# ScalarE's splits that are prepared behind a visit's turnings, queued behind the copies of the turned blocks (hybrid SSD and forgetting-attention layer)

## The chip, the cores and the metric

The kernel runs on one core of a Trainium2 chip. The metric is the device time of one execution in microseconds (us). Five engines work side by side, each with an instruction queue of its own: TensorE (PE, with its weight loads shown apart as PEld), VectorE (DVE), ScalarE (ACT), GpSimd (POOL) and SyncE (SP), which here only issues DMAs. ACT and POOL issue DMAs too. Engines wait for each other through semaphores. The order of the instructions within each queue is fixed when the program is built: a scheduler with a model of the instructions' times plays the program through and puts the instructions in the order in which they come up in that play.

## The reference

One decoder layer on 1024 tokens of width 1024, all in float32, with an SSM branch and an attention branch that share one input projection:

```python
h = rmsnorm(x) * pre_g
z_ssm, xbc, dt, q, k, v, f, z_att, g_ssm, g_att = split(h @ w_in)
# branch A: causal convolution, chunked SSD scan, gated group norm -> y_ssm
# branch B, 16 heads of 64, in blocks of 128 queries:
s = q @ k.T / 8 + F[t] - F[s]          # F = cumsum(log_sigmoid(f)), causal
o = softmax(s) @ v
y_att = o * silu(z_att)
merged = sigmoid(g_ssm) * (y_ssm @ w_branch_ssm) + sigmoid(g_att) * (y_att @ w_branch_att)
out = x + rmsnorm(merged @ w_out) * post_g
```

## The kernel before

**The projections are one long stream.** Every large product (input columns, the two branch matrices, `w_out`) is cut into pairs of units (`Pair`), and each pair is computed by seven half-size products instead of eight, with sums and differences of blocks as operands. One such product is a *step*: twelve matmuls of 128x128 by 128x512, six to each *half-step*. A matmul takes fp32 through two pieces: a high part that ACT makes by copying (`AF.Copy`) and a low part that DVE makes by subtracting the high part. This is what the text calls a *split*. The weights' split is `Pair.split` (ACT at line 351, DVE at line 352, tile `wop`, four buffers). The split of the other operand is `Operands.split` (ACT at 277 or 280, DVE at 278 or 281, tiles `x0h`, `x0l` and so on).

**`Stream` deals the steps out.** `Stream.half()` (line 530) issues one half-step. When the half begins a step, it first calls `ahead(False)`, which prepares the weights of the step three places on (`prepare`, line 522: sums on DVE or POOL, then the split). After the half, each operand set under construction gets a call of `some()` (lines 556 to 560), which fetches blocks and splits those that have landed. Between `hold()` and `release()` these calls are put aside and made later.

**Attention runs between the half-steps.** There are 48 *visits* (`for m in range(6 * NK)`): eight pairs of heads, six visits each. A visit has these parts, and PE takes them in just this order, since its instructions are all kept in program order: the scores (`scores`, tile `s` in PSUM); the weighted sums of the visit before (`weighted`, tile `av`); one or two half-steps "ahead"; the turnings (`turned`, line 1475: PE transposes the probabilities `ex` into PSUM tiles `pt`); and one or two half-steps "behind" (three in the last visit). On the other engines the visit has DVE's addition of the forget term with a row minimum (line 1467, `ex` and `nm`), ACT's exponentials (1471), and the copies of the turned blocks from PSUM into `p` (ACT at 1510, one of four on DVE at 1508 for the first six pairs of heads). `weighted` reads `p`. Scores and turned blocks share one ring of four PSUM buffers (tag `s`), so the next visit's scores need the copies of this visit to be done.

**What sets ACT's order.** Three things bear on it. Instructions under `tc.high_priority()` (the copies at 1510, the exponentials, `Pair.keep` at 404, `give` at 412) go first among those that are ready in the scheduler's play. Instructions under `pin` stay in program order among themselves; the exponentials and the operands' splits are pinned, the weights' splits and the copies are not. And a buffer must be free: a weights' split takes one of four `wop` buffers, and so comes up when the step four places earlier has left PE.

The pass over a visit, cut to the calls that order the work (lines 1648 to 1681):

```python
for one in made:
    weighted(*one)
...
stream.release()
...
stream.halves(ahead)
...
made = turned(hp, g, list(end(m - 1)))
...
stream.hold()
stream.halves(behind)
```

Of the kernel before, what the change touches and what calls it, by code (L numbers as in the profile page):

```python
# [11 lines left out]
AF = mybir.ActivationFunctionType  # L12
# [74 lines left out]
def hybrid_layer(ctx: ExitStack, tc, a, out):  # L87

    nc = tc.nc
# [366 lines left out]
    class Stream:  # L456
# [6 lines left out]
        def __init__(self, pairs, double, last):  # L463
            self.pairs = pairs
            for n, p in enumerate(pairs):
                p.bank, p.other = (pj, "be"[n % 2]), (pjx, "d") if n < double else (pj, "c")

                p.between = n < double or n >= last

            p, q, r = pairs[0:3]  # L470
            self.steps = [(p, 1), (q, 1), (p, 2), (q, 2)] + [(p, n) for n in (6, 5, 7, 4, 3)]
            self.steps += [(q, 6), (q, 5), (q, 7), (r, 1), (q, 4), (q, 3)]
            for n in range(2, last):
                p, nxt = pairs[n], pairs[n + 1]
                self.steps += [(p, i) for i in ((2, 6, 5, 7) if n < double else (6, 2, 7, 5))] + [(nxt, 1)]
                self.steps += [(p, 4), (p, 3)] if n + 1 < last else [(p, 3), (p, 4)]

            a, b, c, d, e, f, g, h = pairs[last:]
            self.steps += [(a, 5), (a, 6), (a, 7), (b, 1), (a, 2), (a, 4), (a, 3)]
            for p, nxt in ((b, c), (c, d), (d, e)):  # L480
                self.steps += [(p, 2), (p, 6), (p, 5), (p, 7), (nxt, 1), (p, 4), (p, 3)]
            self.steps += [(f, 1), (e, 2), (e, 6), (e, 5), (e, 7), (f, 2), (e, 4), (e, 3)]
            self.steps += [(f, 6), (f, 5), (f, 7), (g, 1), (f, 4), (f, 3)]
            self.steps += [(g, 2), (g, 6), (g, 5), (g, 7), (h, 1), (g, 4), (g, 3)]
            self.steps += [(h, 6), (h, 5), (h, 7), (h, 2), (h, 3), (h, 4)]
            self.following = {p: n.ops for p, n in zip(pairs, pairs[1:]) if n.ops is not p.ops}
            self.building = []
            self.chores, self.line = [], []
            self.held = None
            self.count = 0  # L490
            self.at = 0
            self.run = None
            self.waiting = []
            self.loads = [(p, names) for p in pairs for names in (("a11", "a12"), ("a21", "a22"))]
            self.loaded = []
            self.load_next()
# [23 lines left out]
                self.prepare(p, which)  # L520

        def prepare(self, p, which):
            p.prepare(which)
            self.load_more()

        def after(self, halves, fn):

# [2 lines left out]
        def half(self):  # L530
            if self.run is None:
                if self.at == len(self.steps):
                    return False
                p, which = self.steps[self.at]
                if which == 7 and p.ops is ops_a and "merged" not in fin:
                    return False
                if p.ops is ops_a and not all(p.ops.ready(OPERAND[which].strip("-"), j) for j in range(KH)):
                    return False
                self.ahead(False)
                for ops in self.building:  # L540
                    ops.some(OPERAND[which])
                self.run = p.do(which)
                next(self.run)
            else:
                for _ in self.run:
                    pass
                self.run = None
                p, which = self.steps[self.at]
                if p in self.following:
                    ops = self.following[p]  # L550
                    if ops not in self.building:
                        self.building.append(ops)
                    ops.open(OPERAND[which])
                self.ahead(True)
                self.at += 1
            for ops in self.building:
                if self.held is None:
                    ops.some()
                else:
                    self.held.append(ops)  # L560
            for chores in (self.chores, self.line):
                if chores:
                    chore = chores.pop(0)
                    if chore:
                        chore()
            self.count += 1
            for w in self.waiting:
                w[0] -= 1
            for w in [w for w in self.waiting if w[0] <= 0]:
                self.waiting.remove(w)  # L570
                w[1]()
            return True
# [4 lines left out]

        def release(self):
            held, self.held = self.held or [], None
            for ops in held:  # L580
                ops.some()

        def do_chores(self):
            while self.chores:
# [550 lines left out]
    with tc.tile_pool(name="pro", bufs=1, reuse_waits="tile", side="right") as pro, tc.tile_pool(  # L1135
# [53 lines left out]
        stream = Stream(order + late + ends, len(order) + 3, len(order) + len(late) + 4)  # L1189
# [105 lines left out]
    with tc.tile_pool(name="att", bufs=1, reuse_waits="tile", side="right") as ap, tc.tile_pool(  # L1295
# [177 lines left out]
        def turned(hp, g, sent):  # L1473

            pair, h = GROUPS[g]
            bs = list(range(4 * h, min(4 * h + 4, pair[0] + 1)))
            made = {}  # L1480
            order = bs[-1:] + bs[:-1] if sent else bs
            tiles = {b: pp.tile([P, HALF], F32, tag="s", bufs=4, name="pt") for b in order}
            banks = {b: tiles[b].rearrange("p (e t c) -> p e t c", e=2, t=2) for b in order}

            def turn_one(b, e, t):
                turn(banks[b][:, e, t, :], ex[:, e, 1 - t, b % 4 * P : b % 4 * P + P])

            for e in range(2):
                for b in order:
                    turn_one(b, e, 1)  # L1490
            for b in order:
                bank, first = banks[b], max(b - pair[1], 0)
                if sent and b == bs[-1]:
                    assert first == 1
                    for hd, which in sent:
                        hd.turn(which, tiles[b])
                if not first:
                    for e in range(2):
                        turn_one(b, e, 0)
                if sent and b == bs[-1]:  # L1500
                    for hd, which in sent:
                        hd.send(which, tiles[b])
                p = ap.tile([P, 2, 2, P], F32, tag="p", bufs=4, name="p")
                to, src = (x[:, :, first:, :] for x in (p, bank))
                with tc.high_priority():

                    if b % 4 == 1 and hp < NK - 2:
                        nc.vector.tensor_copy(to, src)
                    else:
                        nc.scalar.activation(to, src, AF.Copy)  # L1510
                made[b] = (hp, g, b, first, p)
            return [(*made[b], b == bs[0], b == bs[-1]) for b in bs]

# [126 lines left out]
        for m in range(6 * NK + 1):  # L1640

            if m < 6 * NK:
                hp, g = divmod(m, 6)
                if not g:
                    heads[hp] = Heads(hp)
                for u in range(2):
                    scores(hp, g, u)
            for one in made:
                weighted(*one)
            for hd, which in end(m - 1):  # L1650
                hd.free(which)
            if m == 6 * NK:
                stream.release()
                heads[NK - 1].out(2)
                break
            for hd, which in end(m - 2):
                if hd.last and which:
                    hd.out(which)
            for fn in deferred:
                fn()  # L1660
            deferred.clear()
            stream.release()
            for hd, which in end(m):
                hd.settle(which)
            ahead, behind = room(m)
            stream.halves(ahead)

            for hd, which in end(m):
                hd.scale(which)
                hd.load_gates(which)  # L1670
            loads(m)
            made = turned(hp, g, list(end(m - 1)))
            for hd, which in end(m - 2):
                if not hd.last or not which:
                    hd.out(which)
            if m == 6 * NK - 1:
                tp = pp.tile([P, HALF], F32, tag="s", bufs=4, name="tp")
                heads[hp].turn(2, tp)
                heads[hp].send(2, tp)
            stream.hold()  # L1680
            stream.halves(behind)
            for hd, which in end(m if m == 6 * NK - 1 else m - 1):
                hd.take(which)
# [59 lines left out]
```

## Time and profile before

| what | value |
| --- | --- |
| median of 3 runs | 1290.88 us (1290.15 to 1292.31) |
| the profiled execution, its own time | 1291.84 us |
| its span, first to last instruction | 1290.1 us |
| mean granted TensorE clock | 0.996 |
| attention's 48 visits | from 686.8 to about 1135 us of the span |

The profiled execution is 0.96 us (0.07%) above the median of the runs, and 1.7 us of its time lie outside its span. In the profile, "busy" leaves out the time in which an instruction waits; "idle before" a group is what its engine waited, with the releaser that ended most of it. A matmul's end is modelled, so PE counts as busy from one matmul to the next where they follow closely. The timeline merges equal neighbours into one row (x4 is four instructions) and gives the start, the length, the engine, the line, and the tiles as output<-input.

### The profile page before, as it was taken

The page shows a single profiled execution, that of the slowest core. Times are in us where ns is not written, and L with a number is a line of the kernel's source. Part 1 is how long each engine was busy: PE and PEld are TensorE (multiplying, and loading weights), DVE is VectorE, ACT ScalarE, POOL GpSimd, SP SyncE. Part 2 cuts the span into 40 slices and gives each one's busy share as a digit, 9 for nine tenths or more (in the row PEclk, how much of TensorE's full clock was granted, in tenths as well). Part 3 has the DMA queues.
Part 4 walks back from the last instruction along what each step waited for, and adds up shares of the span by engine and source line. Part 5 has one row for each costly group of instructions (what it writes and reads, how often), then busy time and mean ns, then how long its engine had stood idle before and what let it go on. Part 6 is the DMA issues. An engine that isn't in the chain of part 4 may idle for free.

```text
span 1290.1 us, 20992 instructions
## 1 busy us (share of the span) xinstructions
PE 1255.2 (97%) x7054; PEld 987.4 (77%) x7054; DVE 1005.1 (78%) x1994; ACT 795.6 (62%) x1738; POOL 258.8 (20%) x250
## 2 busy tenths in 40 slices
PE   5999999999999999999999999999999999899997
PEld 3688888787888888888877777777777776678886
DVE  7988886987788978997767567666798767776975
ACT  7745665556665665566556666666786567644754
POOL 4000440013300330124101121110001102146052
PEclk9999999999999999999999999999999999999999
DMA  8232552646336533653365666667787568556932
GB/s 297 72 113 76 154 154 90 190 150 182 131 110 201 186 126 105 217 168 119 132 204 202 200 222 204 206 215 224 259 261 249 199 212 268 191 188 195 360 111 101
DMA packets 153515, 233.57 MB, mean 181 GB/s; under 512 B 15968, under 2 KB 61504, under 8 KB 153408
## 3 DMA queue, kind: packets, MB, share of 16 engines
q1 hardware_dynamic: 137408, 197.14, 48.0%
q10 hardware_dynamic: 11136, 19.11, 3.9%
q0 software_dynamic: 4864, 15.99, 3.2%
q8 instruction: 55, 0.90, 0.3%
q14 instruction: 52, 0.43, 0.1%
HBM read 162.99 MB, written 72.34 MB: 182 GB/s over the span
## 4 chain that ended last, share of the span: by engine, by line
PE 76%; DVE 8%; DMA 7%; ACT 4%; issue 2%; SPq 1%; ACTq 0%; DVEq 0%
PE pb L130 32%; PE pc L130 19%; PE pd L130 6%; PE s L130 5%; PE pt L133 5%; PE av L130 4%; PE yps L130 2%; DVE wop L352 2%; DMA raw<-in_wu 1%; DMA xt<-in_x 1%; PE st L130 1%; DVE sum L357 1%; DMA st_dram<-st 1%; PE tr L133 1%; PE tr_v L133 1%
## 5 line engine op out<-in xcount | busy, mean ns | idle before, releaser
L351 ACT ACTIVATE wop<-sum 128x512 fp32r<-128x512 f32 x180 | 112.5, 626 | 111.4 <-DVE sum L357 52.3
L352 DVE TENSOR_TENSOR wop<-sum,wop 128x512 fp32r<-128x512 f32 x180 | 137.1, 763 | 55.0 <-ACT wop L351 54.0
L1471 ACT ACTIVATE ex<-ex,nm 128x512 f32<-128x512 f32 (+1 forms) x192 | 116.3, 607 | 65.8 <-DVE nm L1467 62.5
L404 ACT ACTIVATE s<-pb 128x512 f32<-128x512 f32 x144 | 85.2, 591 | 99.7 <-PE pb L130 97.7
L130 PE MATMUL pc<-x3h,wop 128*128 128x512 f32 x384 | 130.6, 397 | 1.6 <-DVE th L414 1.3
L130 PE MATMUL pc<-x2h,wop 128*128 128x512 f32 x384 | 130.7, 398 | 0.6 <-DVE u L416 0.6
L130 PE MATMUL pb<-x0h,wop 128*128 128x512 f32 x384 | 131.0, 399 | 0.0
L130 PE MATMUL pb<-x5h,wop 128*128 128x512 f32 x384 | 129.8, 396 | 1.1 <-ACT s L404 1.1
L130 PE MATMUL pb<-x6h,wop 128*128 128x512 f32 x384 | 129.4, 395 | 1.3 <-ACT s L404 1.3
L352 DVE TENSOR_TENSOR wop<-raw,wop 128x512 fp32r<-128x512 f32 x144 | 101.0, 703 | 36.3 <-ACT wop L351 35.9
L130 PE MATMUL pb<-x4h,wop 128*128 128x512 f32 x384 | 129.2, 395 | 0.0
L1467 DVE CUSTOM_DVE_ANT_0 ex<-s,fb 128x512 f32<-128x512 f32 (+1 forms) x192 | 97.2, 552 | 20.0 <-PE s L130 19.9
L351 ACT ACTIVATE wop<-raw 128x512 fp32r<-128x512 f32 x144 | 89.7, 623 | 21.1 <-PE pc L130 13.6
L130 PE MATMUL pd<-x1h,wop 128*128 128x512 f32 x288 | 96.3, 394 | 0.0
L130 PEld LDWEIGHTS pc<-x3h,wop 128*128 128x128 f32 x384 | 72.3, 188 | 18.9 <-DVE th L414 1.7
L130 PEld LDWEIGHTS pb<-x5h,wop 128*128 128x128 f32 x384 | 72.1, 188 | 18.7 <-ACT s L404 2.2
L130 PEld LDWEIGHTS pc<-x2h,wop 128*128 128x128 f32 x384 | 72.1, 188 | 18.4 <-issue 2.8
L130 PEld LDWEIGHTS pb<-x6h,wop 128*128 128x128 f32 x384 | 72.1, 188 | 18.2 <-issue 1.9
L130 PEld LDWEIGHTS pb<-x0h,wop 128*128 128x128 f32 x384 | 72.7, 189 | 17.3 <-issue 2.7
L130 PEld LDWEIGHTS pb<-x4h,wop 128*128 128x128 f32 x384 | 72.3, 188 | 17.1 <-issue 2.3
L133 PE MATMUL pt<-ident,ex 128*128 128x128 f32 x576 | 75.4, 274 | 1.6 <-DVE nm L1467 0.6
L130 PE MATMUL s<-k,q 64*128 64x512 f32 (+3 forms) x576 | 73.6, 368 | 2.0 <-ACT p L1510 1.5
(310 smaller groups left out, 2915.8 us busy)
## 6 DMA issues: line engine op xcount, KB each, us to landing
raw<-in_wu SPq DMA_DIRECT2D x128, 256.0 KB
csb<-cs_dram SPq DMA_DIRECT2D x32, 256.0 KB
fb<-f_dram SPq DMA_DIRECT2D x16, 512.0 KB
rb<-st_dram SPq DMA_DIRECT2D x48, 128.0 KB
wd<-in_wo SPq DMA_DIRECT2D x40, 128.0 KB
xt<-in_x SPq DMA_DIRECT2D x8, 512.0 KB
gs_dram<-th ACTq DMA_DIRECT2D x16, 256.0 KB
qh_dram<-th ACTq DMA_DIRECT2D x16, 256.0 KB
```

The source lines that it names most:

```text
L130: return tc.keep_in_program_order(nc.tensor.matmul(*args, **kw))
L133: return tc.keep_in_program_order(nc.tensor.transpose(out_, in_, idn))
L351: nc.scalar.activation(op[:, 0], src, AF.Copy)
L352: nc.vector.tensor_tensor(op[:, 1], src, op[:, 0], ALU.subtract)
L357: self.adds.tensor_tensor(t, x, y, ALU.add)
L404: nc.scalar.activation(s, ps, AF.Copy)
L1467: nc.vector.tensor_tensor_reduce(o, s[e][:, 0:w], fb[hp, h][:, e, 0:w], 1.0, 3.0e38, ALU.add, ALU.min, nm)
L1471: pin(nc.scalar.activation(o, o, AF.Exp, scale=-1.0, bias=nm, accum_out=hd.at(hd.sm, i, h, e)))
```

## The change

`Stream` gets a field `front`. In `turned`, each copy that goes to ACT is noted there, so after the turnings of a visit `front` is that visit's last copy on ACT. `Stream.behind()` opens `tc.issue_after(front)`: every instruction that is written inside it on the same engine as `front`, which is ACT, gets an ordering edge to it. That is no semaphore and no wait on the chip; it only keeps the scheduler from putting the instruction ahead of the copy in ACT's queue. Three places are wrapped: the preparation of weights (`prepare`), the calls of `some()` on operands that are not held, and the held ones when they are released. At the end of attention `front` is cleared. The list of held calls holds functions instead of objects. Nothing is computed otherwise, and no instruction, DMA or buffer is added or taken away.

```diff
@@ Stream.__init__
             self.held = None
+            self.front = None
@@ Stream
         def prepare(self, p, which):
-            p.prepare(which)
+            with self.behind():
+                p.prepare(which)
             self.load_more()
+
+        def behind(self):
+
+            return nullcontext() if self.front is None else tc.issue_after(self.front)
@@ Stream.half
             for ops in self.building:
                 if self.held is None:
-                    ops.some()
+                    with self.behind():
+                        ops.some()
                 else:
-                    self.held.append(ops)
+                    self.held.append(ops.some)
@@ Stream.release
             held, self.held = self.held or [], None
-            for ops in held:
-                ops.some()
+            for fn in held:
+                with self.behind():
+                    fn()
@@ turned
                     else:
-                        nc.scalar.activation(to, src, AF.Copy)
+                        copy = nc.scalar.activation(to, src, AF.Copy)
+                        stream.front = copy.ins
@@ the loop over the visits
             if m == 6 * NK:
+                stream.front = None
                 stream.release()
```

## The prediction

> **What bounds the kernel now.** The page comes first: the span, then the engines' shares.
>
> ```profile
> span 1290.1 us, 20992 instructions
> PE 1255.2 (97%) x7054; PEld 987.4 (77%) x7054; DVE 1005.1 (78%) x1994; ACT 795.6 (62%) x1738; POOL 258.8 (20%) x250
> ```
>
> PE is idle for 35 us in all. The change reaches only attention, so the next view is the busy time by stretches: pairs of heads 1 and 3 (counted from 0), then 4, then 7, then a short stretch at the end of pair 7. After the stretch and its length stand the busy time of each engine with its instructions, the granted clock and the DMAs.
>
> ```profile
> core 0: us, PE busy (x) PEld busy (x) DVE busy (x) ACT busy (x) POOL busy (x), PEclk, DMA share, GB/s
> 745.83:803.27 57.44, 57.44 (x393) 43.81 (x391) 38.47 (x102) 36.19 (x91) 10.51 (x13) 1.00 0.67 216
> ...
> 860.58:917.89 57.31, 57.31 (x394) 43.84 (x392) 38.53 (x105) 38.78 (x96) 6.87 (x9) 1.00 0.69 223
> 917.89:969.38 51.49, 50.85 (x357) 37.98 (x355) 46.46 (x122) 43.07 (x107) 2.16 (x4) 1.00 0.83 270
> ...
> 1073.09:1135.00 61.91, 55.69 (x345) 39.69 (x344) 48.14 (x117) 42.20 (x105) 9.54 (x13) 0.94 0.66 216
> ...
> 1130.60:1134.00 3.40, 3.40 (x14) 1.90 (x13) 2.27 (x5) 1.74 (x4) 0.00 (x0) 0.53 0.23 78
> ```
>
> In pairs 1 and 3 PE is busy for all of the stretch, and the two agree within 0.13 us: PE runs at its own pace there, and nothing that ACT does earlier can shorten them. What PE loses lies in pair 4 (0.64 us) and above all in pair 7 (6.22 us). Third come PE's waits (and its weight loads') between 660 or 675 and 1140 us: who waited for whom, total, times, longest.
>
> ```profile
> PE tp L133 <- DVE ns L1376: 3.3, 1, 3.3
> PE s L130 <- ACT p L1510: 1.5, 3, 1.1
> ...
> PEld s L130 <- ACT p L1510: 5.4, 12, 1.5
> ```
>
> The second and third row are what the change is about: scores that wait for the copies to empty a PSUM buffer. The matmuls waited 1.5 us for that, the weight loads 5.4 us, much of which passes while earlier matmuls still run.
>
> **The change part by part.** Only ACT's order can change: nothing is added, so all terms come from places in the queue.
>
> *Operands' splits (L277, L280): nothing.* Those of a visit are written after its exponentials and pinned behind them. The exponentials need scores, and these need the copies of the visit before, whose order the edge is to set; so the timeline has, in each of the 47 transitions, the last copy on ACT before the next visit's first exponential (one pair of such rows stands further down, 886.36 and 888.87). The edge repeats an order that stands. It doesn't even reach the costliest case:
>
> ```profile
> 1115.59 0.62 ACT L351 ACTIVATE wop<-sum 128x512 fp32r<-128x512 f32 x1
> 1116.11 1.14 ACT L280 ACTIVATE x3h<-x3l 128x512 fp32r<-128x512 f32 x2
> 1117.93 0.27 ACT L1393 ACTIVATE st<-pt 8x128 f32<-8x128 f32 x1 [0.69 <-PE pb L130]
> 1118.11 0.36 ACT L1510 ACTIVATE p<-pt 128x256 f32<-128x256 f32 x1
> ...
> 1118.52 1.09 PE L130 MATMUL s<-k,q 64*128 64x256 f32 x6 [1.09 <-ACT p L1510]
> ```
>
> This is visit 46, with PE's longest wait for a copy, 1.09 us. The operands' splits ahead of `st`, and the weights' split between them, were written before this visit's turnings, when `front` still was visit 45's last copy. They stay.
>
> *Weights' splits prepared in the half-steps behind (L351).* I went through the timeline visit by visit. PE's order shows which half-steps behind begin a step, and the n-th split belongs to the n-th step. 31 preparations fall behind the turnings, 48 ahead; none of the 48 stands before the copies of the visit before. Of the 31, 21 started before their visit's last copy on ACT. These are what moves; the other ten run after the copies already. The first and the last of the 21, and one from pair 1:
>
> ```profile
> 692.70 0.62 ACT L351 ACTIVATE wop<-raw 128x512 fp32r<-128x512 f32 x1
> 693.23 1.33 ACT L1510 ACTIVATE p<-pt 128x512 f32<-128x512 f32 x3
> ...
> 759.64 0.63 ACT L351 ACTIVATE wop<-sum 128x512 fp32r<-128x512 f32 x1 [1.08 <-PE pc L130]
> ...
> 760.90 0.58 ACT L1510 ACTIVATE p<-pt 128x512 f32<-128x512 f32 x1
> ...
> 1105.96 0.62 ACT L351 ACTIVATE wop<-sum 128x512 fp32r<-128x512 f32 x1
> 1106.48 0.20 ACT L1368 ACTIVATE dd<-dd 128x8 f32<-128x8 f32 x1
> 1106.58 2.04 ACT L1510 ACTIVATE p<-pt 128x512 f32<-128x512 f32 x4
> ```
>
> The split at 759.64 lies in a hole in which ACT had nothing else, and is over 0.6 us before the copy: moving it gains nothing. In ten of the 21 a copy (or `st`, or `dd`) follows directly, as at 693.23, and could start up to 0.5 us earlier. It gains time only where PE waits for it. In nine of the ten the scores behind run in their usual time (within 0.1 us). The tenth is visit 45; the scores behind it stand here under those of the same group in pair 1:
>
> ```profile
> 781.97 0.96 PE L130 MATMUL s<-k,q 64*128 64x512 f32 x6
> ...
> 783.70 0.65 PE L130 MATMUL av<-p,v 128*64 128x256 f32 x4
> ...
> 1107.41 1.24 PE L130 MATMUL s<-k,q 64*128 64x512 f32 x6
> ...
> 1109.51 1.95 PE L130 MATMUL av<-p,v 128*64 128x256 f32 x16
> ```
>
> From the scores' start to `av` it takes 1.73 us in pair 1 and 2.10 us behind visit 45: a stall of 0.37 us, which copies 0.5 us earlier would cover. **Gain: 0.4 us.**
>
> *What the moved splits meet.* Each can start when the last copy ends: for the first of the rows above at 694.56 instead of 692.70, 1.9 us later, for the last at 1108.62, 2.7 us later. Its DVE half (L352) comes later with it. The weights are used three steps on, behind 36 matmuls at least; at pair 3's pace (57.31 us for 394) that is 5.2 us, an estimate that leaves out what stands between steps, so PE doesn't wait for weights. On ACT the split falls into the hole between copies and exponentials. On DVE it can fall ahead of the next row minima (L1467), on which exponentials and turnings hang. The tightest place is visits 20 and 21:
>
> ```profile
> 886.36 0.60 ACT L1510 ACTIVATE p<-pt 128x512 f32<-128x512 f32 x1 [0.37 <-ACT st L1393]
> 888.87 0.72 ACT L1471 ACTIVATE ex<-ex,nm 128x512 f32<-128x512 f32 x1 [1.92 <-DVE nm L1467]
> ...
> 887.54 0.69 DVE L381 TENSOR_TENSOR raw<-raw 128x512 f32<-128x512 f32 x1
> 888.15 0.68 DVE L1467 CUSTOM_DVE_ANT_0 ex<-s,fb 128x512 f32<-128x512 f32 x1
> ...
> 891.62 0.19 ACT L1471 ACTIVATION_READ_ACCUMULATOR ex<-ex,nm 128x1 f32 x1
> ...
> 892.01 1.25 PE L133 MATMUL pt<-ident,ex 128*128 128x128 f32 x10
> ```
>
> The moved split would run from 886.96 to 887.6, its DVE half beside L381. If that goes before L1467, the minima come 0.6 us later, and of that the exponentials' lead over the turnings (891.71 to 892.01) covers 0.30: a loss of 0.3 us. Ends for this term: 0 if the scheduler puts DVE's half behind the minima (they have priority), and 0.3 us. I take 0.2. The order of DVE and SP follows the scheduler's play too, and the trace can't show that. The nearest rows bound it: SP holds back loads of weights for L352, and DVE stands for ACT's half.
>
> ```profile
> SPq L344 <- DVE wop L352: 28.0, 10, 7.4
> ...
> DVE wop L352 <- ACT wop L351: 39.2, 29, 3.4
> ```
>
> Some 2.7 us at most (the longer of the two moves) is added to each of those ten waits, and loads of `q`, `k` and `rb` stand behind them on SP; PE waits for none of them today but the last `rb`. DVE's 39.2 us may shrink or move, and PE has no wait from them in pairs 0 to 6. I take 0 for both, with 2.7 us of loss and 1 us of gain as ends.
>
> *Sum:* -0.4 + 0.2 = -0.2 us. On the profiled execution that is 1291.84 - 0.2 = 1291.6. That execution stands 0.96 us above the median of the runs, 1290.88, so on the median the sum makes **1290.7 us**, the number I give.
>
> *A rule against my reading.* The stretch of pair 3 has PE 100% busy, and PEld 43.84 of 57.31 us. The Trainium skill (Perfetto Trace Analysis, Identifying the Most-Contended Engine) says that a busy share of matmuls isn't a good measure of how near PE is to its limit and that the share of weight loads is one. By it, PE could have 13 us to give in each pair, and ten copies 0.5 us earlier might be worth 5 us: 1285.9. By the rows it is 0.4, since equal stretches with no wait leave nothing for a copy to release. I go by the rows.
>
> **The rivals.**
>
> *Slower: the moved halves land in the next visit's chain.* DVE's half (0.69) before the minima and ACT's (0.62) before the exponentials delay the turnings by up to 1.31 us. What covers it is the exponentials' lead over the turnings. It is below 0.76 us behind nine of the 21 (visits 2, 8, 12, 14, 20, 27, 36, 38, 45), the first and the last of these:
>
> ```profile
> 719.19 0.19 ACT L1471 ACTIVATION_READ_ACCUMULATOR ex<-ex,nm 128x1 f32 x1
> ...
> 719.95 1.25 PE L133 MATMUL pt<-ident,ex 128*128 128x128 f32 x10
> ...
> 1113.41 0.19 ACT L1471 ACTIVATION_READ_ACCUMULATOR ex<-ex,nm 128x1 f32 x1
> ...
> 1114.25 1.03 PE L133 MATMUL pt<-ident,ex 128*128 128x128 f32 x8
> ```
>
> The lead there is 0.67 and 0.75 us (the next instruction overlaps the read by 0.1). It decides from where both halves come before the last minimum. Price: 9 x (1.31 - 0.67) = 5.8 us, so 1296.7; with half of them 1293.8. For it: DVE is 90% busy in pair 4. Against it: minima and exponentials have priority, and ACT's holes mostly hold the split.
>
> *Faster: the end of pair 7 closes up.* PE stands 3.3 us for `ns` (the first row of its waits), which DVE reaches only after it has waited for `rb`:
>
> ```profile
> 1127.40 0.69 DVE L1431 TENSOR_TENSOR o<-o,rb 128x512 f32<-128x512 f32 x1 [2.99 <-DMA rb<-st_dram]
> ```
>
> That DMA hangs on the `st` of 1117.93. In the stretch from 1130.60 the granted clock is 0.53: just behind the gap PE works at half speed for 3.4 us, a loss of 1.7 us. If the copies of visit 45 and a new order of DVE bring `st` 1 us forward and the gap closes by as much, the half-speed stretch may vanish with it: 0.4 + 1.0 + 1.7 = 3.1 us, so 1287.8. The Trainium skill (TensorE: Matmul & The Clock Gate, What's actually happening) has the clock halved after an idle window of about 3.4 us and given back after a busy one of that length; the trace agrees, with 3.3 us idle and 3.4 us slow. Against it: what holds `st` is not an ACT split that moves.
>
> *Slower by transfers:* a held-back weight load delays the `rb` or `q` behind it in pair 7, up to 2.7 us: 1293.6.
>
> *The edge binds nothing that matters* (the copies start earlier, and PE gives it back at the gap): 1290.9, inside the forecast.
>
> **How the numbers follow.** What can be told from no change is 0.2%, 2.6 us. Forecast, with the last rival: 0.34; its own range 1288.3 to 1293.4. Faster: 0.30. Slower in the next visit's chain: 0.27; by transfers: 0.09. That makes 0.30 faster, 0.34 the same, 0.36 slower. The range goes from 1286.2, below the faster case, to 1296.7, the full price of the slower one.
>
> **What would show it.** Right: no L351 prepared behind stands ahead of the visit's last L1510; the stretches of pairs 1 and 3 keep 57.3 us; the time from scores to `av` behind visit 45 falls to about 1.75 us; the row of PE waiting for `p` keeps its 1.09 us. Slower is shown by new waits of `pt` for L1471 or L1467 in pairs 0 to 6; faster by a shorter wait of `tp`. Wrong is the forecast if PE's order or the length of a stretch before pair 4 changes, or if the stage after attention moves: it has the same instructions and may still be put in another order.

## The result, and the profile after

| | median | runs | ratio, 95% interval |
| --- | --- | --- | --- |
| before, measured beside it | 1290.59 us (1287.28 to 1294.19) | 15 | |
| changed kernel | 1288.41 us (1286.99 to 1290.55) | 15 | 0.9982 [0.9974, 0.9991] |

The change makes the kernel 2.2 us faster (0.18%). Runs of one kernel spread over 3.6 to 7 us, so one profile is never enough to tell such a difference; the medians of many runs do, and the profiles say where to look. In the rows shown, line numbers from 1000 on are 8 higher after than before.

The first view is the page's span and shares, then the busy time by stretches (columns as before: pair 3, pair 7, and the 3.4 us behind the gap at its end), then PE's waits from 675 to 1140 us, all of the changed kernel.

```profile
span 1288.2 us, 20979 instructions
PE 1255.0 (97%) x7054; PEld 987.1 (77%) x7054; DVE 1006.2 (78%) x1994; ACT 795.4 (62%) x1738; POOL 259.5 (20%) x250
```

```profile
859.60:917.00 57.40, 57.40 (x396) 43.89 (x393) 39.44 (x107) 38.61 (x95) 7.17 (x9) 1.00 0.67 222
...
1073.00:1133.60 60.60, 54.67 (x343) 38.95 (x342) 46.28 (x117) 41.86 (x105) 9.39 (x13) 0.94 0.66 223
1128.70:1132.10 3.40, 3.40 (x14) 1.84 (x13) 2.04 (x4) 2.27 (x5) 0.00 (x0) 0.50 0.12 44
```

```profile
PE tp L133 <- DVE ns L1384: 3.3, 1, 3.3
PE pt L133 <- DVE nm L1475: 1.5, 3, 0.9
PE pt L133 <- ACT ex L1479: 0.9, 3, 0.4
PE pb L130 <- ACT s L404: 0.7, 1, 0.7
PE s L130 <- DVE p L1516: 0.3, 1, 0.3
```

PE's busy time is the same. Pair 3 has no idle time, as before. What is gone is the row of scores that waited for ACT's `p` (1.5 us before, 1.09 us of it at visit 46). What is new is 1.5 us of turnings that wait for the row minima (0.6 us before, and all three are in pair 7: from 675 to 1070 us there is no such row). The gap at the end of pair 7 (`tp`) and the half-speed stretch behind it are still there. Another row of before that is gone, 1.3 us in which `pc` waits for `th` (L414) at 675.7 us, lies ahead of attention. It comes and goes between kernels with the same queues up to there (1.6 us in E7 below, none in E9).

Below, a visit's length is the time from the start of its scores to the start of the next scores; for the last one, visit 47, to the turned norms `tp`. From visit 7's scores to visit 24's both traces take 162.04 us, and from visit 0's to visit 42's 383.76 before and 383.87 after. Within the latter, visit 0 takes 9.07 us before and 10.16 after, and pair 4 takes 51.53 and 50.63; a second profile of the changed kernel (E1 below) has 9.36 and 52.03, so neither difference can be put down to the change. What is left is pair 7. There the two profiles differ by 0.8 of the 1.9 us between their spans, which is too little to go by alone.

### The profile page after: what moved, and what is told of

The parts are those of the page before. It is cut to its first block, busy times and chain, and to the rows that moved or that the text cites. A ratio compares the mean times of both kernels' runs of the same rounds, so it can differ in the third digit from the quotient of the medians.

```text
span 1288.2 us, 20979 instructions
## 1 busy us (share of the span) xinstructions
PE 1255.0 (97%) x7054; PEld 987.1 (77%) x7054; DVE 1006.2 (78%) x1994; ACT 795.4 (62%) x1738; POOL 259.5 (20%) x250
## 4 chain that ended last, share of the span: by engine, by line
PE 75%; DVE 9%; DMA 8%; ACT 3%; issue 3%; SPq 1%; POOL 0%; DVEq 0%; ACTq 0%; POOLq 0%
PE pb L130 31%; PE pc L130 18%; PE pd L130 5%; PE pt L133 5%; PE s L130 5%; PE av L130 5%; PE yps L130 2%; DVE wop L352 2%; DMA raw<-in_wu 1%; DVE sum L357 1%; DMA xt<-in_x 1%; DVE xs L779 1%; DMA xr<-in_x 1%; PE st L130 1%; DVE ex L1475 1%
## 5 line engine op out<-in xcount | busy, mean ns | idle before, releaser
L352 DVE TENSOR_TENSOR wop<-sum,wop 128x512 fp32r<-128x512 f32 x180 | 138.0, 768 | 57.5 <-ACT wop L351 56.7
L352 DVE TENSOR_TENSOR wop<-raw,wop 128x512 fp32r<-128x512 f32 x144 | 104.1, 724 | 36.5 <-ACT wop L351 36.0
L130 PEld LDWEIGHTS pc<-x2h,wop 128*128 128x128 f32 x384 | 72.6, 189 | 18.1 <-issue 2.8
L133 PEld LDWEIGHTS pt<-ident,ex 128*128 128x128 f32 x576 | 66.8, 141 | 13.7 <-ACT ex L1479 4.4
```

What stands on the lines that cost most here:

```text
L130: return tc.keep_in_program_order(nc.tensor.matmul(*args, **kw))
L133: return tc.keep_in_program_order(nc.tensor.transpose(out_, in_, idn))
L352: nc.vector.tensor_tensor(op[:, 1], src, op[:, 0], ALU.subtract)
```

## The experiments

The table has all the profiles of pair 7 side by side (us, from the timeline's starts of `s<-k,q` and `tp<-ident,ns`), with the ratio of the times to the kernel before.

| kernel | 42 and 43 | 44 | 45 | 46 | 47 | sum | ratio, 95% interval |
| --- | --- | --- | --- | --- | --- | --- | --- |
| before | 19.21 | 8.11 | 9.56 | 11.10 | 10.90 | 58.89 | |
| after | 19.49 | 6.77 | 12.55 | 9.58 | 9.71 | 58.10 | 0.9982 [0.9974, 0.9991] |
| E1 the change again | 19.35 | 6.75 | 12.86 | 9.59 | 9.78 | 58.33 | 0.9975 [0.9965, 0.9985] |
| E2 edge in pairs 0 to 3 | 19.21 | 10.38 | 9.54 | 11.13 | 10.48 | 60.75 | 1.0003 [0.9993, 1.0013] |
| E3 edge in pairs 4 to 6 | 19.21 | 8.37 | 10.79 | 11.12 | 10.38 | 59.86 | 0.9993 [0.9982, 1.0005] |
| E4 edge in pair 7 | 19.73 | 6.76 | 12.42 | 9.59 | 8.55 | 57.05 | 0.9979 [0.9969, 0.9990] |
| E5 edge at visit 42 | 19.16 | 6.76 | 12.56 | 9.59 | 9.56 | 57.64 | 0.9993 [0.9978, 1.0007] |
| E6 edge at visit 45 | 19.24 | 7.30 | 11.33 | 9.61 | 9.86 | 57.34 | 0.9985 [0.9973, 0.9998] |
| E7 DVE alone, visit 43 | 19.42 | 6.75 | 12.92 | 9.59 | 10.31 | 58.98 | 0.9998 [0.9987, 1.0009] |
| E8 late operands | 20.10 | 6.76 | 9.56 | 9.61 | 9.65 | 55.69 | 1.0002 [0.9992, 1.0012] |
| E9 DVE alone, visit 45 | 19.77 | 7.15 | 10.81 | 9.98 | 9.32 | 57.03 | 0.9982 [0.9970, 0.9993] |
| E10 GpSimd's add alone | 19.67 | 6.77 | 10.99 | 9.99 | 10.61 | 58.04 | 0.9980 [0.9970, 0.9990] |
| E11 change, `b21` late | 19.40 | 6.77 | 9.36 | 10.15 | 8.63 | 54.31 | 0.9944 [0.9930, 0.9957] |
| E12 DVE alone, both | 19.22 | 6.75 | 10.14 | 9.95 | 8.83 | 54.88 | 0.9972 [0.9960, 0.9984] |

### Where: E1 to E4

E1 is the changed kernel unaltered. The other three keep the edge only in some pairs of heads:

```diff
-                        stream.front = copy.ins
+                        stream.front = copy.ins if hp < 4 else None
```

with `hp < 4` in E2, `4 <= hp < 7` in E3, `hp == 7` in E4.

> The changed kernel again, on the chip of the three runs beside it. If the 0.18% is real, the ratio to the kernel before is 0.997 to 0.999 (2.3 us less). If it is chance, 0.9995 to 1.001. In the profile the time from the scores to av behind visit 45, counted outside the half-speed stretch, is 1.75 us by my reading.

> The edge only where the front copy belongs to pairs of heads 0 to 3 (13 of the 21 moved splits). My theory: PE has no wait there, so ratio 1.000 within 0.0008 and strips of 57.3 us for pairs 1 to 3. Rival (the copies are worth time everywhere, since matmul busy time hides PE's slack): most of the gain, ratio 0.9985 or less.

> The edge only where the front copy belongs to pairs 4 to 6 (6 or so of the moved splits). Theory that the gain sits in visit 45 of pair 7: ratio 1.000. Rival theory that it sits in pair 4, where DVE is 90% busy and the waits of scores for copies lie: 0.8 to 1.0 us less, ratio 0.9992, and the strip of pair 4 falls from 51.5 to 50.6 us.

> The edge only where the front copy belongs to pair 7 (visits 42 and 45). Theory that the gain sits in visit 45: all of it, ratio 0.998 to 0.9992, and no scores that wait for copies in visits 43 and 46. Rival theory of pair 4: 1.000.

E4 has the whole gain (0.9979 beside E1's 0.9975), and E2 and E3 are no different from the kernel before. The three effects add up to E1's: +0.0003 - 0.0007 - 0.0021 = -0.0025. So most of the moved splits change nothing that can be measured, and the six visits of pair 7 make the difference. The profiles agree: pair 7 takes 58.9 to 60.8 us in the three without the edge there (before, E2, E3) and 57.1 to 58.3 in the three with it (after, E1, E4), in the mean 2.0 us less.

### Which visit: E5, E6, E7

When the edge moves a split on ACT, the scheduler's play comes out otherwise on DVE too. With the edge at visit 42, the low part of these weights (L352) and a product of another unit (L1070, `times`) come ahead of `zr<-o,rb` in visit 43. With the edge at visit 45, L352 comes behind the small operations of the softmax, and `th<-s,pc` (L418) and the product L1070 behind it each come ahead of one operand split more. E5 and E6 have the edge at one visit; E7 has no edge at all and makes only the new order of DVE in visit 43 (two loads of `rb` move up by one load on SP with it).

```diff
E5 (E6 has (7, 3))
-                        stream.front = copy.ins
+                        stream.front = copy.ins if (hp, g) == (7, 0) else None
E7
         def behind(self):
-            return nullcontext() if self.front is None else tc.issue_after(self.front)
+            return nullcontext()
@@ Heads.out
-                    pin(nc.vector.tensor_tensor(z, o, self.rb[n], ALU.mult))
+                    with (tc.issue_after(stream.low) if self.hp == 6 else nullcontext()), (tc.issue_after(stream.times) if self.hp == 6 else nullcontext()): pin(nc.vector.tensor_tensor(z, o, self.rb[n], ALU.mult))
```

`stream.low` and `stream.times` are the latest L352 and L1070.

> The edge stands in force only for what is made in the half-steps behind visit 42's first copies (the first visit of pair 7). Against the kernel before, ScalarE has one weights' split (L351) moved behind visit 42's copies; VectorE has the low part of those weights (L352) and the product with the unit (L1070) moved from behind zr<-o,rb (L1433, which waits for the rb transfer) to ahead of it. Theory 1 (VectorE's order around the rb transfer): visit 44's scores to visit 45's take 6.8 us as in the changed kernel (8.1 before), and the time has a ratio of 0.998 to 0.999. Theory 2 (ScalarE, copies of the turned blocks come earlier): visit 42's own scores-to-av is shorter by a split, 0.4 us, and visit 44 keeps 8.1 us; ratio 0.9997. Theory 3 (the gain is behind visit 45): ratio 1.000, visit 46 to 47 keeps 11.1 us.

> The edge stands in force only for what is made behind visit 45's first copies. Theory 1: visit 44 to 45 keeps 8.1 us; what is left is at most the score wait at visit 46 (1.1 us before), ratio 0.999 to 1.000. Theory 2: score to av behind visit 45 falls from 2.1 to 1.75 us, ratio 0.9997. Theory 3 (the product with the unit, L1070, ahead of the splits of x5l and x3l frees the slot of st earlier, and visit 46 to 47 falls from 11.1 to 9.6 us): ratio 0.998 to 0.999.

> No edge at all on ScalarE: its order, TensorE's and GpSimd's are those of the kernel before, instruction for instruction. On VectorE alone, L352 and L1070 of visit 43 are put ahead of zr<-o,rb (L1433); the planner then issues the two rb loads on SP one x3l load earlier. Theory 1: visit 44 to 45 takes 6.8 us and the time is that of the changed kernel, ratio 0.998 to 0.9985; the copies on ScalarE had no part in it. Theory 2 (ScalarE's copies) and theory 3 (visit 45): ratio 1.000, visit 44 to 45 8.1 us.

Theory 1 was half right and its conclusion wrong. The timeline of DVE in visit 43, before and then after:

```profile
1086.25 0.23 DVE L1384 SCALAR_TENSOR_TENSOR ns<-dd,sm 128x4 f32<-128x4 f32 x2
1088.90 0.69 DVE L1425 TENSOR_TENSOR zr<-o,rb 128x512 f32<-128x512 f32 x1 [2.43 <-DMA rb<-st_dram]
1089.51 0.69 DVE L352 TENSOR_TENSOR wop<-sum,wop 128x512 fp32r<-128x512 f32 x1
1090.11 0.69 DVE L1062 SCALAR_TENSOR_TENSOR th<-th 128x512 f32<-128x512 f32 x1
1090.71 2.37 DVE L278 SCALAR_TENSOR_TENSOR x4l<-x4l,x4h 128x512 fp32r<-128x512 f32 x2
1093.00 0.41 DVE L1467 CUSTOM_DVE_ANT_0 ex<-s,fb 128x256 f32<-128x256 f32 x1
```

```profile
1086.24 0.66 DVE L352 TENSOR_TENSOR wop<-sum,wop 128x512 fp32r<-128x512 f32 x1
1086.82 0.68 DVE L1070 SCALAR_TENSOR_TENSOR th<-th 128x512 f32<-128x512 f32 x1
1087.42 1.32 DVE L1392 SCALAR_TENSOR_TENSOR ns<-dd,sm 128x4 f32<-128x4 f32 x2
1088.65 0.68 DVE L1433 TENSOR_TENSOR zr<-o,rb 128x512 f32<-128x512 f32 x1
...
1090.46 0.41 DVE L1475 CUSTOM_DVE_ANT_0 ex<-s,fb 128x256 f32<-128x256 f32 x1
```

Before, DVE stands 2.43 us for the `rb` transfer with two pieces of ready work behind it; after, that work, 1.2 us, fills the wait. Another 1.1 us lies in the two `x4l` between `zr` and the minima: they take 2.37 us before, beside an add on POOL from 1090.34 to 1091.93, and 1.28 us after, where the add has run ahead of them (1087.04 to 1088.64). What an add on POOL does to DVE is the subject of the next section. Against visit 42's scores (1070.53 and 1069.95) the minima come 22.47 and 20.51 us later, 2.0 us earlier after. Visit 44 then takes 6.75 to 6.77 us in all eight kernels with this order, and 6.77 to 10.38 us in the six without, depending on when `rb` lands in that run; in E2 (10.38) the clock adds to it, which is 0.50 from 1097.56 to 1100.97 us. E7 has it too, with ACT untouched. But E7's time is that of the kernel before (0.9998), and E5's can't be told from it: visit 45 gives the gain back. ACT in visit 45, before and then after:

```profile
1100.15 0.63 ACT L280 ACTIVATE x1h<-x1l 128x512 fp32r<-128x512 f32 x1 [1.50 <-DMA x1l<-ya_dram]
```

```profile
1100.09 0.63 ACT L280 ACTIVATE x1h<-x1l 128x512 fp32r<-128x512 f32 x1 [3.08 <-DMA x1l<-ya_dram]
1100.62 0.62 ACT L280 ACTIVATE x5h<-x5l 128x512 fp32r<-128x512 f32 x1
1101.14 0.71 ACT L1479 ACTIVATE ex<-ex,nm 128x512 f32<-128x512 f32 x1
```

The visit's exponentials stand behind an operand split whose load lands when it lands (1100.1 in both). Who comes earlier waits longer. That is not all that visit 45 gives back. In the five profiles in which it takes 12.4 us or more (after, E1, E4, E5, E7) it contains a half-speed stretch of 3.41 us; in the other nine it has at most 0.4 us of one. Visit 45 of the changed kernel and of E10 (below), columns as in the stretches by time above:

```profile
1096.21:1108.76 12.55, 10.95 (x56) 7.86 (x56) 8.84 (x25) 8.39 (x19) 2.10 (x2) 0.86 0.72 249
```

```profile
1096.26:1107.25 10.99, 9.37 (x55) 6.49 (x54) 7.59 (x20) 7.19 (x17) 2.20 (x3) 1.00 0.80 275
```

In both, `x1h` starts 3.9 us behind the visit's scores, and PE is idle for 1.6 us. Of the 3.0 us that visit 45 takes longer than before, 1.6 us are thus the clock, and 1.4 us come with the load, as far as one profile of each can tell. What is left is E6: the edge at visit 45 is worth 0.9985 by itself.

### What it is in visit 45: E9, E10, E12

DVE and POOL behind visit 45, in the kernel before:

```profile
1106.61 0.69 DVE L352 TENSOR_TENSOR wop<-sum,wop 128x512 fp32r<-128x512 f32 x1 [0.31 <-ACT wop L351]
...
1107.22 0.16 DVE L1379 TENSOR_TENSOR sm<-sm,dd 128x8 f32<-128x8 f32 x1
1107.40 1.27 POOL L373 TENSOR_TENSOR sum<-sum,raw 128x512 f32<-128x512 f32 x1 [5.77 <-DVE sm L1379]
...
1107.42 1.28 DVE L1381 TENSOR_TENSOR sm<-sm 128x4 f32<-128x4 f32 x1
...
1110.15 0.68 DVE L1467 CUSTOM_DVE_ANT_0 ex<-s,fb 128x512 f32<-128x512 f32 x1
```

`sm<-sm` adds four numbers per partition, and takes 1.28 us. Of its 16 instances in this profile 15 take 0.15 to 0.17 us, and this is the only one that starts beside an add on POOL; it ends with that add. The add (L373) forms the next weights in the buffer that L352 reads, so it can start only behind L352. Where L352 stands in DVE's queue decides beside what the add runs. In the changed kernel L352 comes last:

```profile
1105.98 0.16 DVE L1387 TENSOR_TENSOR sm<-sm,dd 128x8 f32<-128x8 f32 x1
1106.18 0.16 DVE L1389 TENSOR_TENSOR sm<-sm 128x4 f32<-128x4 f32 x1
...
1108.41 0.69 DVE L352 TENSOR_TENSOR wop<-sum,wop 128x512 fp32r<-128x512 f32 x1 [0.53 <-ACT wop L351]
...
1109.20 1.28 POOL L373 TENSOR_TENSOR sum<-sum,raw 128x512 f32<-128x512 f32 x1 [9.21 <-DVE wop L352]
...
1109.88 0.69 DVE L1475 CUSTOM_DVE_ANT_0 ex<-s,fb 128x512 f32<-128x512 f32 x1 [0.78 <-PE s L130]
```

Now the minima run beside the add and keep their 0.69 us; they read the scores from PSUM. The Trainium skill (SBUF — State Buffer, Who interferes with whom) says that a VectorE instruction with two inputs in SBUF contends with a GpSimd instruction that reads SBUF, through a port pair that is an exclusive lock, and that one with at most one SBUF input doesn't contend, outside the modes that use two ports. The trace agrees on both sides, with 1.28 us and 0.69 us.

E9 makes the new DVE order of visit 45 alone, E12 that of visits 43 and 45; in both ACT's order is that of the kernel before in every place. E10 leaves all orders as before and only makes POOL's add wait, through a copy of one column (0.18 us) that needs `zr`.

```diff
E9, E12 (E12 with E7's edges as well): no edge on ACT, and in Pair.split
+                with (tc.issue_after(stream.zr) if stream.zr is not None and which == 6 else nullcontext()):
                     nc.vector.tensor_tensor(op[:, 1], src, op[:, 0], ALU.subtract)
E10: no edge on ACT, and in Pair.prepare
-                self.adds.tensor_tensor(self.s2, self.s2, r["a12"], ALU.add)
+                with (tc.issue_after(stream.tiny()) if stream.zr is not None else nullcontext()): self.adds.tensor_tensor(self.s2, self.s2, r["a12"], ALU.add)
@@ Stream
+        def tiny(self): (z, o), self.zr = self.zr, None; return nc.gpsimd.tensor_copy(o[:, 0:1], z[:, 0:1]).ins
```

`stream.zr` is the last `zr<-o` (L1440) in E9 and E12; in E10 it holds the tiles of that operation in visit 45.

> No edge on ScalarE; its order, and those of TensorE, GpSimd and SP, are those of the kernel before. On VectorE alone the order is the one that the edge at visit 45 gave: the low part of the weights (L352) behind zr<-o (L1440), and the product with the unit (L1070) ahead of two splits of operands. Theory A (VectorE's order): GpSimd's add, which waits for L352, no longer runs beside the sums of the softmax, sm<-sm (L1389) takes 0.17 us and not 1.28, visit 46 to 47 takes 9.6 us (11.1 before), ratio 0.998 to 0.999. Theory B (the copies of the turned blocks on ScalarE): score to av behind visit 45 stays at 2.1 us, visit 46 to 47 stays at 11.1, ratio 0.9995 to 1.0005.

> The kernel before in the order of every engine, but for one copy of one column on GpSimd that waits for zr<-o of visit 45 and holds GpSimd's add (L373) behind it. Theory A (the add and VectorE's small operation exclude each other): sm<-sm (L1389) takes 0.17 us, the minima of visit 46 come 1.1 us earlier against its scores, visit 46 to 47 takes 10.0 us, ratio 0.999 to 0.9995. Rival (VectorE is slow there for another reason, or the add then holds up the next operation): 1.28 us stays or comes back at another operation, visit 46 to 47 stays at 11.1 us, ratio 1.000.

> VectorE's order of visits 43 and 45 as in the changed kernel, ScalarE's order as in the kernel before in every place. Theory A (all of the gain is VectorE's order): from visit 42's scores to the last turned norms 57.5 to 58 us as in the changed kernel (58.9 to 60.7 without it), ratio 0.9975 to 0.9985. Theory B (ScalarE's copies have the larger part): ratio 0.999 to 1.000.

All three came out on theory A's side. E10 gained more than expected (0.9980 for 0.999 to 0.9995), E12 a little more (0.9972, and 54.88 us where 57.5 to 58 was expected), and visit 46 of E9 took 9.98 us and not 9.6, of which more below. In E10 the same operations in the same order show what the add alone cost:

```profile
1106.44 0.69 DVE L352 TENSOR_TENSOR wop<-sum,wop 128x512 fp32r<-128x512 f32 x1 [0.31 <-ACT wop L351]
1107.05 0.16 DVE L1387 TENSOR_TENSOR sm<-sm,dd 128x8 f32<-128x8 f32 x1
1107.25 0.17 DVE L1389 TENSOR_TENSOR sm<-sm 128x4 f32<-128x4 f32 x1
...
1108.88 0.68 DVE L1475 CUSTOM_DVE_ANT_0 ex<-s,fb 128x512 f32<-128x512 f32 x1
```

From L352 to the minima it takes 2.44 us, where the kernel before took 3.54. Visit 46 falls from 11.1 to 10.0 us in all three, and each has a gain that can't be told from the change's (0.9982 and, in E1, 0.9975): 0.9982, 0.9980, 0.9972. A kernel whose ACT order is that of before thus has the gain of a change that orders ACT. The changed kernel's own visit 46 would not have shown it: E5 and E7 keep DVE's order and the long `sm<-sm` in visit 45 (1.27 and 1.28 us), and their visit 46 takes 9.59 us all the same. With visit 45 at half speed PE is late, and the minima come 1.2 us behind its scores, where they come 2.74 us behind them in the kernel before.

Visit 46 is 1.1 us shorter, and the time of E9 and E10 falls by 2.3 to 2.6 us. From visit 46's scores to the norms the profile of E9 is 2.7 us shorter than that of before, that of E10 1.4. What goes beyond visit 46 lies in visit 47, which depends on the same chain through the product L1062 (L1070 after). Before, the product, `rb`'s issue, and SP's wait ahead of it (timelines of DVE and SP, and the waits of SP from 1116 to 1128 us):

```profile
1117.16 0.69 DVE L1062 SCALAR_TENSOR_TENSOR th<-th 128x512 f32<-128x512 f32 x1
```

```profile
1123.35 1.09 SPq L1400 DMA_DIRECT2D rb<-st_dram  x2
```

```profile
SPq L1400 <- DMA ms_dram<-th: 1.3, 1, 1.3
```

After, the product, `st` and `rb`'s issue (DVE, ACT, SP):

```profile
1116.30 0.69 DVE L1070 SCALAR_TENSOR_TENSOR th<-th 128x512 f32<-128x512 f32 x1
...
1117.07 0.27 ACT L1401 ACTIVATE st<-pt 8x128 f32<-8x128 f32 x1
...
1121.98 1.09 SPq L1408 DMA_DIRECT2D rb<-st_dram  x2
```

`st`, `rb` and the products share one ring of four buffers. In both kernels `st` starts 0.08 us behind the product's end (1117.93 and 1117.07), as it does within 0.01 us in eleven of the other twelve profiles (not in E11); then come the copies that the scores need. And the last thing that `rb` waits for on SP is the buffer that the product's store to `ms_dram` reads (1.3 us before, 2.3 after). The product comes 9.75 us behind visit 46's scores before, 7.54 after; `rb` is issued 15.94 us behind them before (1123.35), 13.22 after (1121.98). From visit 46's scores to the norms it takes 21.5 to 22.0 us in the three profiles whose pair 7 is as before in every queue (before, E2, E3), and 18.1 to 20.6 in all others.

### What visit 45 gives back: E8, E11

E8 splits all operands of the second chain two steps of the planner later, E11 those of `b21` (`x1`) one step later, so that visit 45's exponentials stand ahead of the split that waits. Both contain the change.

```diff
E8
-                    if name == only or only is None and n < most and self.at[name, j] < self.step - 4:
+                    if name == only or only is None and n < most and self.at[name, j] < self.step - (6 if self is ops_a else 4):
E11
-                    if name == only or only is None and n < most and self.at[name, j] < self.step - 4:
+                    if name == only or only is None and n < most and self.at[name, j] < self.step - (5 if self is ops_a and name == "b21" else 4):
```

> The changed kernel, and the operands of the second chain split six steps of the planner behind their load and not four. In the changed kernel visit 45's exps stand on ScalarE behind x1h<-x1l, which waits for its load: visit 45 to 46 takes 12.5 us where it was 9.6 before. Theory 1 (that wait gives back 3 us of what visits 44 and 46 gain): visit 45 to 46 falls to 9.6 to 10.5 us, and the time to 1286 to 1287.5 us, ratio 0.996 to 0.9975, unless the splits that come later hold the chain at the end. Rival (the 3 us are the half-speed clock and not the load): visit 45 to 46 stays at 12 us and the time at 1288.4.

> The changed kernel, and of the second chain's operands those of b21 alone (x1) split five steps behind their load and not four, so that visit 45's first exps stand ahead of the x1h<-x1l that waits for its load, while x3's splits keep their place. If that wait is what visit 45 gives back: visit 45 to 46 takes 9.6 to 10.5 us (12.5 in the changed kernel) and the time is 1286 to 1287.5 us, ratio 0.9965 to 0.9975. Rival (the end of the pair hangs on the transfers of rb, whose slot the product's store frees): visit 45 to 46 is shorter but the turned norms at the pair's end come when they came, ratio 0.998.

In both, visit 45 falls from 12.5 to 9.6 and 9.4 us. With the wait for the load the half-speed stretch in the visit is gone too, so the wait was the cause of what visit 45 gives back, and the clock a part of its price. E8 still missed its time, by 4 us: its splits of `x3` come too late, PE waits for them at the pair's end, and a half-speed stretch of 10.24 us lies there (from 1125.16).

```profile
PE tp L133 <- DVE ns L1384: 3.6, 1, 3.6
PE pc L130 <- ACT x3h L280: 2.7, 1, 2.7
```

Behind the norms E8 needs 164.86 us to the end of the span, where the kernel before needs 160.72. E11 leaves `x3` alone. It is the best version: 1284.46 us (1283.35 to 1285.59, 6 runs) against 1291.66 before on the same chip, 7.2 us faster, and faster than the change. Its PE waits, and ACT in visit 45, where the load no longer stands ahead of the exponentials:

```profile
PE tp L133 <- DVE ns L1384: 1.6, 1, 1.6
...
PE pt L133 <- ACT ex L1479: 0.4, 2, 0.2
PE pt L133 <- DVE nm L1475: 0.3, 1, 0.3
```

```profile
1096.61 0.62 ACT L280 ACTIVATE x5h<-x5l 128x512 fp32r<-128x512 f32 x1
1098.67 0.72 ACT L1479 ACTIVATE ex<-ex,nm 128x512 f32<-128x512 f32 x1 [1.45 <-DVE nm L1475]
...
1102.50 0.61 ACT L280 ACTIVATE x1h<-x1l 128x512 fp32r<-128x512 f32 x1
```

Visit 45 came out a little under the 9.6 to 10.5 us expected, and the time 1.5 us under its expected range, for the gap of `tp` halved as well. Three things go together in E11 and were not taken apart: the load behind the exponentials, the product L1070 ahead of one operand split more than in the changed kernel, and the clock, 0.998 or 0.999 in its runs and 0.995 to 0.998 in those of before.

## Why the prediction was right, and where not

The number, 1290.7 us, was 2.3 us too high; the measured 1288.4 lies in the range and at the lower edge of the forecast's own (1288.3). The direction of the sum was right, but by luck: its gain, 0.4 us, is less than a fifth of the measured 2.2 us, and no run shows that it reaches the kernel's time at all. The number lies in the range because the range was wide, not because its terms were the right ones.

- **Most moved splits change nothing: right.** Visits 7 to 23 take the same time to 0.01 us, and E2 is no different from before.
- **Visit 45, a gain of 0.4 us from earlier copies: right in the visit, not shown in the time.** From scores to `av` it takes 1.73 us in the changed kernel (2.10 before):

```profile
1108.76 0.96 PE L130 MATMUL s<-k,q 64*128 64x512 f32 x6
...
1110.49 1.30 PE L130 MATMUL av<-p,v 128*64 128x256 f32 x10
```

That alone is no proof, since E7 has 1.73 us too, with ACT's order of before and PE late. But E6 and E9 differ in ACT's order alone, and visit 46 takes 9.61 and 9.98 us: 0.37 us. The time doesn't keep it: from visit 46's scores to the norms E6 takes 19.47 us and E9 19.30, and the ratios are 0.9985 and 0.9982. That is the prediction's last rival, in which PE gives the earlier copies back at the gap.
- **Visits 20 and 21, a loss of 0.2 us: wrong, there is none.** Visits 20 and 21 take 8.13 and 9.82 us in both, to 0.01 us; the lower end, 0, held.
- **"The order of DVE and SP follows the scheduler's play ... I take 0 for both, with 2.7 us of loss and 1 us of gain as ends": this step failed.** DVE's order was the change's main effect: alone it is worth 0.9982 in visit 45 (E9) and 0.9972 in both visits (E12), or 2.3 and 3.6 us, where the end of the range allowed 1 us of gain. The trace of before had shown its place: the 1.28 us of `sm<-sm` stand in the chain from visit 45 to visit 46. I had gone through ACT's queue row by row, and through DVE's only for its waits; an operation that is blocked while it runs shows no wait, it is just long.
- **"The row of PE waiting for `p` keeps its 1.09 us": wrong.** I read that what holds `st` is not an ACT split that moves. That is so, but what holds it, the product L1062, moved.
- **The faster rival (1287.8) was nearest in the number**, and in the place, the end of pair 7. Its price was made up otherwise: in the profile after, the gap is still 3.3 us and the half-speed stretch is still there; they come earlier.
- **The rule of weight loads (1285.9) is not borne out:** pair 3, with PEld busy for 43.89 of 57.40 us, didn't shorten.
- **Slower rivals: none came.** From 675 to 1070 us PE has one new wait of `pt`, 0.3 us for an exponential, and SP's waits for L352 became shorter (30.5 us before, 23.1 after, from 675 to 1140 us). What did cost is a case that was not among them: an earlier visit 44 that only waits longer for a load in visit 45, with a half-speed stretch behind the wait.

What stays open: why `rb` and `x1` land when they do. They differ between profiles of kernels whose queues are the same up to there (visit 44 takes 8.11 us before, 7.15 in E9 and 6.77 in E10; the split of `x1` starts 4.24 us behind visit 45's scores in E7 and 3.06 in E12), and no run varied it. Nor was it tried to give `st` or `rb` a buffer of its own.

## What to carry to other kernels

An ordering edge on one engine is an edge for the scheduler, and the order of every engine follows it: compare all queues, not only the one that was edited, and try the other engines' new order by itself. Look for operations that take several times their usual length with no wait beside them, and see what runs on the neighbour engine. When a gain stops at the next transfer's arrival, move what waits for that transfer out of the queue of what doesn't; here that was worth more than the change itself.

## What the runs showed of the hardware

- An add of 128x512 on GpSimd stretches a VectorE operation on 4 columns from 0.16 to 1.28 us (E10 takes the coincidence away in visit 45, and the stretch with it; its one long `sm<-sm`, 1.25 us at 835.43, lies beside another add, from 835.16 to 836.66). In visit 43 the 1.1 us move from `x4l` (2.37 us for two before, 1.28 after) to `ns<-dd,sm` (0.23 and 1.32), where they lie in the wait for `rb`.
- TensorE's half-speed stretches lie on a grid. In the records of the granted clock in attention each is 3.41 us long or a multiple of it, and their distances are too: 1120.2 and 1130.4 before (three times 3.41), 1104.8 and 1128.7 after (seven times). The grid's place differs from run to run, so the same stall costs a half-speed stretch in one run and not in another. In visit 45 of the changed kernel it lies in one window of the grid (PE is busy for 54% of 1101.42 to 1104.84, and half speed follows); the same stall in E10 lies in two (82% and 71% from 1099.33 on, at full speed behind). In all fourteen profiles, each half-speed stretch of attention starts behind a window in which PE is busy for 61% or less, and two such windows (54% in E3, 49% in E4) have none behind them. From visit 42's scores to 1140 us the profiles have between 3.4 us (E4) and 10.2 us (E8) at half speed. That fits the free-running window of the Trainium skill (TensorE: Matmul & The Clock Gate, Part 1: The HAM clock gate). A window that is idle throughout, as in the prediction's faster rival, was not needed. The grid may be a part of the spread of 3.6 to 7 us; that was not tried.
